# Strassen output projection: contiguous column halves and 4 KB rows for the weight sums

## The chip, the cores and the metric

One core of a Trainium2 chip runs the whole program once per launch. The metric is device time in microseconds (us). Before the change three runs took 857.10, 857.14 and 857.69 us, with a median of 857.14 us. TensorE runs at its 2.4 GHz level; the profile lists the granted clock as 0.998 of it over the span.

## The reference, cut to what matters

One decoder layer on 512 tokens of width 2048, all in float32. `y_att` comes from an attention, `y_conv` from a convolution module; the change touches only the projection that follows.

```python
h = _rmsnorm(x, g_pre)
proj = h @ w_in
...
y = jnp.concatenate([y_att, y_conv], axis=-1) @ w_out      # (512, 2048) @ (2048, 2048)
x = x + _rmsnorm(y, g_post)
```

## The kernel before

**Precision.** A float32 matrix is split into a high part `h_...` (rounded by ScalarE, L104) and a low part `l_...` (the rest, by VectorE, L105). A product then takes three matmuls, high by high, high by low and low by high (L351 to L353, L1089 to L1091).

**Steps.** The weights are taken in steps of 1 MB each. For a step SyncE issues the load into a `raws` buffer (two of them), ScalarE makes the high part, VectorE the low part, and TensorE then reads both. VectorE's instruction is the last reader of the raw buffer, so the load two steps later waits for it. Loads, splits and matmuls of all steps are ordered by the program's priorities; within an engine instructions run in order.

**The output projection by Strassen.** `w_out` is seen as 2 x 2 blocks. Rows fall into a first and a last half (`r`), columns into two classes (`c`). Before, class `c` holds column groups of 512 that alternate: group `2 * p + c` for `p` = 0, 1 (`w_block`, L978). Seven products `q` replace eight; their order is `ORDER` = 1, 5, 6, 3, 2, 7, 4 (L976). Products 1, 3 and 2 take a block of `w_out` as it is (`PLAIN`, L512). Products 5, 6, 7 and 4 take a sum of blocks (`SUMS`, L511). Each product has four steps `(p, kg)`: `p` is the column group, `kg` the half of the rows. So there are 28 steps of 24 matmuls, 16 of them on sums. A load is named `r_w` with the digits of q, p and kg, as `r_w501`. In product 4 the step (1, 0) only holds its weights, and step (1, 1) multiplies with both, 12 matmuls of each in turn (L1101 to L1121).

**The sums.** They are made by DMA alone, in DRAM tiles `ws`. `plan_sums` (L514) makes for each of 5, 6, 7, 4 four copies (L528), from `w_out` or from an earlier sum's tile, and then four accumulating transfers (L524), one for each `(p, kg)`. A transfer from `w_out` takes 512 rows of 2 KB. GpSimd issues them. `sum_next` (L536) ties each one behind the latest matmul, so that they spread over the steps from `SUMS_FROM` = 20 on; none is released in the gate steps called `z`. A sum's tile is 128 partitions x 8 KB, and `load_w` (L1003) brings it into the raw buffer in one transfer whose rows are 8 KB.

**The end.** `product_done` (L1026) combines the products into four column pieces `e` of 512 for each group `m` of 128 tokens; `finish` (L1135) scales them and adds the residual. For m < 3 two of the four pieces are scaled on ScalarE and added on GpSimd (L1174, L1175), the other two are done on VectorE (L1177); SyncE stores the four in order of `e` (L1180), between the last loads of weights.

Of the kernel before, what the change touches and what calls it, by code (L numbers as in the profile page):

```python
# [11 lines left out]
F32 = mybir.dt.float32  # L12
F32R = mybir.dt.float32r
AF = mybir.ActivationFunctionType
ALU = mybir.AluOpType

P = 128
S = 512
# [35 lines left out]
def hybrid_layer(  # L54
# [15 lines left out]
    nc = tc.nc  # L70
# [10 lines left out]
    dram = ctx.enter_context(tc.tile_pool(name="dram", bufs=1, space=bass.MemoryType.DRAM))  # L81
# [90 lines left out]
    rows = []  # L172
# [338 lines left out]
    SUMS = {5: ((0, 0), (0, 1)), 6: (5, (1, 1)), 4: (6, (1, 0)), 7: ((0, 1), (1, 1))}  # L511
    PLAIN = {1: (0, 0), 3: (1, 1), 2: (1, 0)}  # L512

    def plan_sums(name, order, pairs, block):  # L514

        made, todo = {}, deque()
        for q in order:
            base, more = SUMS[q]
            for accumulate in (False, True):
                for p in range(pairs):  # L520
                    for kg in range(2):
                        def go(q=q, base=base, more=more, accumulate=accumulate, p=p, kg=kg):
                            if accumulate:
                                return nc.gpsimd.dma_start(  # L524
                                    made[q, p, kg], block(*more, p, kg), accum_op=ALU.add
                                )
                            made[q, p, kg] = dram.tile([P, 4, S], F32, name=f"{name}{q}{p}{kg}")
                            return nc.gpsimd.dma_start(  # L528
                                made[q, p, kg],
                                made[base, p, kg] if isinstance(base, int)  # L530
                                else block(*base, p, kg),
                            )
                        todo.append(go)
        return made, todo
# [429 lines left out]
    yg, xr, gp = {}, {}, {}  # L964
    ssy = const.tile([P, NT, 4], F32, name="ssy")
# [11 lines left out]

    def w_block(r, c, p, kg):  # L978
        rows = slice((r * 2 + kg) * S, (r * 2 + kg + 1) * S)
        cols = slice((2 * p + c) * S, (2 * p + c + 1) * S)  # L980
        return w_out[rows, cols].rearrange("(k p) c -> p k c", p=P)

    w_sum, w_sumq = plan_sums("ws", (5, 6, 7, 4), 2, w_block)

    sumq = deque()
    while w_sumq:
# [16 lines left out]
    def load_w(q, p, kg):  # L1003
        name = f"w{q}{p}{kg}"
        n = ORDER.index(q)
        if (p, kg) == (1, 0) and n + 1 < len(ORDER):
            make_form(ORDER[n + 1])
        ahead = min(2000, tc.cur_priority - floor[0])
        with tc.high_priority(offset=ahead):
            raw = raws.tile([P, 4, S], F32, tag="raw", name=f"r_{name}")  # L1010
            nc.sync.dma_start(raw, w_block(*PLAIN[q], p, kg) if q in PLAIN else w_sum[q, p, kg])
            hi, lo = parts(name)
            split(hi, lo, raw)
        return hi, lo
# [3 lines left out]
    def keep(tag, m, e, name):  # L1018
        yg[m, e] = t2(f"{name}{m}_{e}")
        return yg[m, e]  # L1020
# [5 lines left out]
    def product_done(q, p, i):  # L1026

        m1, m2 = i, 2 + i
        a, b = banks.get(("a", p, i)), banks.get(("b", p, i))
        tt = nc.vector.tensor_tensor  # L1030
        if q == 1:
            nc.scalar.copy(keep("s1", m1, 2 * p, "s1_"), a)
        elif q == 5:
            nc.scalar.copy(keep("t5", m2, 2 * p + 1, "t5_"), b)
        elif q == 6:
            nc.scalar.copy(keep("r", m1, 2 * p + 1, "r_"), a)
        elif q == 3:
            c12 = yg[m1, 2 * p + 1]
            tt(out=c12, in0=b, in1=c12, op=ALU.subtract)
            done(m1, 2 * p + 1)  # L1040
        elif q == 2:
            c11 = yg[m1, 2 * p]
            tt(out=c11, in0=banks["c", p, i], in1=c11, op=ALU.add)
            done(m1, 2 * p)
        elif q == 7:
            c22 = yg[m2, 2 * p + 1]
            tt(out=c22, in0=c22, in1=a, op=ALU.subtract)
            done(m2, 2 * p + 1)
        else:
            e = 2 * p  # L1050
            c21 = keep("c21", m2, e, "c21_")
            square_sum(m2, e, a)
            scaled = partial(nc.vector.tensor_tensor, out=c21, in0=a, in1=gp[e], op=ALU.mult)
            if p == 0:
                scaled()
                sum_most(m2)
                finish(m1, 2, lambda: None)
            else:
                with tc.manual_schedule(engines={mybir.EngineType.DVE}):
                    finish(m2, 2, scaled)  # L1060
            return
        if q == 2 and p == 1:
            sum_most(m1)

    def done(m, e):
        square_sum(m, e, yg[m, e])
        nc.vector.tensor_tensor(out=yg[m, e], in0=yg[m, e], in1=gp[e], op=ALU.mult)
# [57 lines left out]
    def sum_most(m):  # L1125

        v = const.tile([P, 1], F32, name=f"fv{m}")
        nc.vector.tensor_tensor(out=v, in0=ssy[:, m, 0:1], in1=ssy[:, m, 1:2], op=ALU.add)
        nc.vector.tensor_tensor(out=v, in0=v, in1=ssy[:, m, 3:4], op=ALU.add)
        nc.vector.tensor_scalar(  # L1130
            out=v, in0=v, scalar1=-0.5 / D, scalar2=-0.5 * RMS_EPS, op0=ALU.mult, op1=ALU.add
        )
        most[m] = v

    def finish(m, left, scaled):  # L1135

        v = most[m]
# [15 lines left out]
        if m == 3:  # L1153

            ps = op2.tile([P, S], F32, tag="o2", name="last")
            diag = fin.tile([P, P], F32, name="diag")
            nc.tensor.matmul(ps, ident, xr[m][:, 0, :], start=True, stop=False)
            nc.scalar.mul(diag, ident, y)
            nc.tensor.matmul(ps, diag, yg[m, 0], start=False, stop=True)
            nc.scalar.copy(yg[m, 0], ps)  # L1160
            nc.scalar.dma_start(of[rows, :S], yg[m, 0])

            pieces = [(1, 0, S // 2), (1, S // 2, S), (3, 0, S), (2, 0, S // 2), (2, S // 2, S)]
            for n, (e, a, b) in enumerate(pieces):
                o = xr[m][:, e, a:b]
                nc.vector.scalar_tensor_tensor(
                    out=o, in0=yg[m, e][:, a:b], scalar=y, in1=o, op0=ALU.mult, op1=ALU.add
                )
                nc.sync.dma_start(of[rows, e * S + a : e * S + b], o)
            return  # L1170
        for e in range(4):
            o = xr[m][:, e, :]
            if e in (1, 3):
                nc.scalar.mul(yg[m, e], yg[m, e], y)  # L1174
                nc.gpsimd.tensor_tensor(out=o, in0=yg[m, e], in1=o, op=ALU.add)  # L1175
            else:
                nc.vector.scalar_tensor_tensor(  # L1177
                    out=o, in0=yg[m, e], scalar=y, in1=o, op0=ALU.mult, op1=ALU.add
                )
            nc.sync.dma_start(of[rows, e * S : (e + 1) * S], o)  # L1180
# [299 lines left out]
```

## Time and profile before

| what | value |
|---|---|
| runs | 857.10, 857.14, 857.69 us (median 857.14) |
| the profiled execution, its own time | 858.71 us |
| its span, first to last instruction | 857.0 us |
| share of the span: TensorE, VectorE, ScalarE, GpSimd | 99%, 77%, 49%, 16% |
| DMA, mean over the span | 228 GB/s, 195.04 MB |
| copies and accumulating transfers from w_out into ws | 24 of 1 MB, 9.4 us from issue to landing (median) |
| loads of ws tiles | 16 of 1 MB |

The profiled execution took 858.71 us where the median of the runs is 857.14; 1.71 us of it lie outside the span. Matmuls are pipelined, so a busy TensorE in these views means that it never ran dry; two matmuls with 512 columns start 0.23 us apart. Idle time of another engine matters only where TensorE waits in turn.

### The profile page before, as it was taken

The numbers are of one execution on the slowest core, as the hardware profiler recorded it, in microseconds if no ns is written. First come the engines' busy times: TensorE is split into PE (matmuls) and PEld (weight loads), VectorE is DVE, ScalarE is ACT, GpSimd is POOL, SyncE is SP. The second block draws the span as 40 slices with busy tenths as digits, with TensorE's granted clock in tenths as the row PEclk, the third lists the DMA queues.
The fourth block names the chain that finished last, engine by engine and source line by source line (L and its number), as shares of the span: only waits on it lengthen the run. The fifth ranks groups of instructions, "written<-read, shape, count | busy, mean of one in ns | idle before, by whom it ended". The sixth has DMA issues, their size and how long they took to land.

```text
span 857.0 us, 9935 instructions
## 1 busy us (share of the span) xinstructions
PE 847.6 (99%) x3872; PEld 702.3 (82%) x3872; DVE 658.5 (77%) x791; ACT 417.3 (49%) x475; POOL 137.6 (16%) x170
## 2 busy tenths in 40 slices
PE   9999999999999999999999999999999999999996
PEld 7888878888888888888888888888888888888885
DVE  5698899777589798997969898468964776458774
ACT  6784222565534342436432535369843356455543
POOL 0111110010130223222121333330000100000031
PEclk9999999999999999999999999999999999999999
DMA  8798989575877879876689887937755995557783
GB/s 317 243 289 196 325 256 234 191 225 196 299 229 209 245 148 215 276 197 196 191 222 188 235 245 159 283 103 289 295 197 197 220 263 205 197 197 260 288 282 102
DMA packets 92278, 195.04 MB, mean 228 GB/s; under 512 B 3702, under 2 KB 46210, under 8 KB 86856
## 3 DMA queue, kind: packets, MB, share of 16 engines
q1 hardware_dynamic: 66688, 120.74, 41.0%
q0 software_dynamic: 22304, 69.21, 33.7%
q10 hardware_dynamic: 3240, 4.46, 1.5%
q8 instruction: 30, 0.49, 0.2%
q14 instruction: 16, 0.13, 0.0%
HBM read 186.01 MB, written 75.50 MB: 305 GB/s over the span
## 4 chain that ended last, share of the span: by engine, by line
PE 91%; DMA 4%; DVE 2%; ACT 2%; issue 0%; POOL 0%; ACTq 0%; DVEq 0%; POOLq 0%
PE za L351 3%; PE za L353 3%; PE a L1089 3%; PE za L352 3%; PE a L1090 3%; PE a L1091 3%; PE k L353 3%; PE k L351 3%; PE k L352 3%; PE u L351 3%; PE u L353 3%; PE u L352 3%; PE q L353 3%; PE q L351 3%; PE q L352 3%; DMA r_q<-in_w_in_dram 2%
## 5 line engine op out<-in xcount | busy, mean ns | idle before, releaser
L410 DVE SCALAR_TENSOR_TENSOR acc<-hg,vec,acc 128x512 f32<-128x512 f32 x240 | 183.1, 763 | 7.2
L105 DVE TENSOR_TENSOR l_w<-r_w,h_w 128x2048 fp32r<-128x2048 f32 x28 | 64.2, 2292 | 43.5 <-ACT h_w L104 43.5
L104 ACT ACTIVATE h_w<-r_w 128x2048 fp32r<-128x2048 f32 x28 | 53.6, 1916 | 43.4 <-DMA r_w<-ws 16.9
L353 PE MATMUL k<-h_hi,l_k 128*128 128x512 f32 x128 | 50.0, 390 | 1.1 <-DVE l_k L105 1.1
L351 PE MATMUL u<-h_hi,h_u 128*128 128x512 f32 x128 | 50.1, 392 | 0.0
L351 PE MATMUL q<-h_hi,h_q 128*128 128x512 f32 x128 | 50.1, 392 | 0.0
L351 PE MATMUL za<-h_hi,h_za 128*128 128x512 f32 x128 | 50.1, 391 | 0.0
L351 PE MATMUL k<-h_hi,h_k 128*128 128x512 f32 x128 | 50.1, 391 | 0.0
L353 PE MATMUL q<-h_hi,l_q 128*128 128x512 f32 x128 | 49.9, 390 | 0.0
L353 PE MATMUL za<-h_hi,l_za 128*128 128x512 f32 x128 | 49.9, 390 | 0.0
L353 PE MATMUL u<-h_hi,l_u 128*128 128x512 f32 x128 | 49.9, 390 | 0.0
L352 PE MATMUL u<-h_lo,h_u 128*128 128x512 f32 x128 | 49.8, 389 | 0.0
L352 PE MATMUL za<-h_lo,h_za 128*128 128x512 f32 x128 | 49.8, 389 | 0.0
L352 PE MATMUL q<-h_lo,h_q 128*128 128x512 f32 x128 | 49.8, 389 | 0.0
L352 PE MATMUL k<-h_lo,h_k 128*128 128x512 f32 x128 | 49.8, 389 | 0.0
L1091 PE MATMUL a<-h_w,f_lo 128*128 128x512 f32 x128 | 49.8, 389 | 0.0
L1089 PE MATMUL a<-h_w,f_hi 128*128 128x512 f32 x128 | 49.8, 389 | 0.0
L1090 PE MATMUL a<-l_w,f_hi 128*128 128x512 f32 x128 | 49.8, 389 | 0.0
L105 DVE TENSOR_TENSOR l_z<-r_z,h_z 128x2048 fp32r<-128x2048 f32 x14 | 32.1, 2291 | 16.3 <-ACT h_z L104 16.3
L105 DVE TENSOR_TENSOR l_v<-r_v,h_v 128x2048 fp32r<-128x2048 f32 x14 | 32.1, 2290 | 15.3 <-ACT h_v L104 15.3
L698 POOL TENSOR_SCALAR_AFFINE_SELECT t<-t 128x128 f32<-128x128 f32 x64 | 33.6, 562 | 54.1 <-ACT t L734 30.1
L104 ACT ACTIVATE h_v<-r_v 128x2048 fp32r<-128x2048 f32 x14 | 26.8, 1916 | 29.6 <-PE g L352 13.2
(381 smaller groups left out, 2238.2 us busy)
## 6 DMA issues: line engine op xcount, KB each, us to landing
ws<-in_w_out_dram POOLq DMA_DIRECT2D x24, 1024.0 KB, 9.4
r_w<-ws SPq DMA_DIRECT2D x16, 1024.0 KB
vs<-in_w_in_dram POOLq DMA_DIRECT2D x12, 1024.0 KB, 12.7
zs<-in_w_in_dram POOLq DMA_DIRECT2D x12, 1024.0 KB, 9.3
r_w<-in_w_out_dram SPq DMA_DIRECT2D x12, 1024.0 KB
r_u<-in_w_in_dram SPq DMA_DIRECT2D x8, 1024.0 KB
r_q<-in_w_in_dram SPq DMA_DIRECT2D x8, 1024.0 KB
r_k<-in_w_in_dram SPq DMA_DIRECT2D x8, 1024.0 KB
```

The costliest lines, as they stand in the source:

```text
L104: nc.scalar.activation(hi, src, AF.Copy)
L105: made = nc.vector.tensor_tensor(out=lo, in0=src, in1=f32(hi), op=ALU.subtract)
L351: nc.tensor.matmul(ps, wh, ah, start=first, stop=False)
L352: nc.tensor.matmul(ps, wh, al, start=False, stop=False)
L353: latest[0] = nc.tensor.matmul(ps, wl, ah, start=False, stop=last).ins
L410: bgq.append(lambda j=j: nc.vector.scalar_tensor_tensor(out=acc, in0=hg[:, j : j + S], scalar=vec[:, ct, j : j + 1], in1=acc, op0=ALU.mult ...
L698: nc.gpsimd.affine_select(out=blk, in_=blk, compare_op=ALU.is_gt, fill=0.0, base=0, pattern=[[-1, P]], channel_multiplier=1,)
L1089: nc.tensor.matmul(ps, fh[:, kk, ts], hi[:, k, :], start=st, stop=False, skip_group_check=True)
L1090: nc.tensor.matmul(ps, fh[:, kk, ts], lo[:, k, :], start=False, stop=False, skip_group_check=True)
L1091: nc.tensor.matmul(ps, fl[:, kk, ts], hi[:, k, :], start=False, stop=en, skip_group_check=True)
```

## The change

The columns of `w_out` are split into the first and the last 1024 instead of alternating groups of 512. Class `c`, group `p` is now the column group `2 * c + p`. A sum over a class is therefore contiguous over 1024 columns, and the four tiles of a sum are cut by rows instead of by `p`: a tile `(part, kg)` holds 256 rows of 4 KB (`w_wide`) in the place of 512 rows of 2 KB. The load of step `(p, kg)` then needs half of each of two tiles, and takes two transfers of 512 KB, each with rows of 2 KB. Column pieces change their numbers: `2 * p + c` becomes `2 * c + p`, in the combining, in the sums of squares and at the end, where GpSimd now adds the pieces 2 and 3 instead of 1 and 3.

```diff
-    def plan_sums(name, order, pairs, block):
+    def plan_sums(name, order, pairs, block, shape=(4, S)):
...
-                            made[q, p, kg] = dram.tile([P, 4, S], F32, name=f"{name}{q}{p}{kg}")
+                            made[q, p, kg] = dram.tile([P, *shape], F32, name=f"{name}{q}{p}{kg}")
...
     def w_block(r, c, p, kg):
         rows = slice((r * 2 + kg) * S, (r * 2 + kg + 1) * S)
-        cols = slice((2 * p + c) * S, (2 * p + c + 1) * S)
+        cols = slice((2 * c + p) * S, (2 * c + p + 1) * S)
         return w_out[rows, cols].rearrange("(k p) c -> p k c", p=P)
 
-    w_sum, w_sumq = plan_sums("ws", (5, 6, 7, 4), 2, w_block)
+    def w_wide(r, c, part, kg):
+
+        first = r * 2 * S + kg * S + part * 2 * P
+        rows = w_out[first : first + 2 * P, c * 2 * S : (c + 1) * 2 * S]
+        return rows.rearrange("(k p) c -> p k c", p=P)
+
+    w_sum, w_sumq = plan_sums("ws", (5, 6, 7, 4), 2, w_wide, (2, 2 * S))
...
-            nc.sync.dma_start(raw, w_block(*PLAIN[q], p, kg) if q in PLAIN else w_sum[q, p, kg])
+            if q in PLAIN:
+                nc.sync.dma_start(raw, w_block(*PLAIN[q], p, kg))
+            else:
+                for part in range(2):
+                    nc.sync.dma_start(
+                        raw[:, 2 * part : 2 * part + 2],
+                        w_sum[q, part, kg][:, :, p * S : (p + 1) * S],
+                    )
...
-            e = 2 * p
+            e = p
...
-                finish(m1, 2, lambda: None)
+                finish(m1, 1, lambda: None)
...
-            if e in (1, 3):
+            if e in (2, 3):
                 nc.scalar.mul(yg[m, e], yg[m, e], y)
                 nc.gpsimd.tensor_tensor(out=o, in0=yg[m, e], in1=o, op=ALU.add)
```

On TensorE, VectorE and ScalarE the same instructions stand in the same order as before. On GpSimd the order is the same too, with other shapes. This is its stretch at the first sums of product 5 (zs is another sum, which is not touched):

```order
 L528 DMA zs_1847<-in_w_in_dram 512x1x512
-L528 DMA ws_1883<-in_w_out_dram 512x1x512
+L528 DMA ws_1883<-in_w_out_dram 256x1x1024
 L528 DMA zs_1901<-in_w_in_dram 512x1x512
-L528 DMA ws_1945<-in_w_out_dram 512x1x512
+L528 DMA ws_1945<-in_w_out_dram 256x1x1024
```

All 24 transfers from w_out change in this way; the 8 copies from one ws tile to another stay as they are.

On SyncE 147 rows become 163. At the loads of product 5 they were (r_w500 is the load of q = 5, p = 0, kg = 0; ws510 the tile of q = 5, second place, kg = 0):

```order
L1011 DMA r_w111_5325<-in_w_out_dram 128x4x512
L1011 DMA r_w500_5357<-ws500_1883 128x2048
L1011 DMA r_w501_5391<-ws501_1945 128x2048
L1011 DMA r_w510_5441<-ws510_2073 128x2048
L1011 DMA r_w511_5475<-ws511_2193 128x2048
```

and are now

```order
L1018 DMA r_w111_5325<-in_w_out_dram 128x4x512
L1021 DMA r_w500_5357<-ws500_1883 128x2x512
L1021 DMA r_w500_5357<-ws510_2073 128x2x512
L1021 DMA r_w501_5392<-ws501_1945 128x2x512
L1021 DMA r_w501_5392<-ws511_2193 128x2x512
L1021 DMA r_w510_5443<-ws500_1883 128x2x512
L1021 DMA r_w510_5443<-ws510_2073 128x2x512
L1021 DMA r_w511_5478<-ws501_1945 128x2x512
L1021 DMA r_w511_5478<-ws511_2193 128x2x512
```

Each load is two transfers, and the first load of a product now reads a tile that only the third one read before.

On SyncE at the loads of product 4, between the stores of the finished rows (xr0, xr1), it was

```order
L1011 DMA r_w400_6127<-ws400_4154 128x2048
L1180 DMA out_0_dram<-xr0_6195 128x512 x2
L1011 DMA r_w401_6165<-ws401_4183 128x2048
L1180 DMA out_0_dram<-xr0_6195 128x512 x2
L1180 DMA out_0_dram<-xr1_6197 128x512
L1011 DMA r_w410_6199<-ws410_4241 128x2048
L1180 DMA out_0_dram<-xr1_6197 128x512 x3
L1011 DMA r_w411_6283<-ws411_4972 128x2048
```

and is now

```order
L1021 DMA r_w400_6139<-ws400_4154 128x2x512
L1021 DMA r_w400_6139<-ws410_4241 128x2x512
L1193 DMA out_0_dram<-xr0_6209 128x512 x2
L1021 DMA r_w401_6178<-ws401_4183 128x2x512
L1021 DMA r_w401_6178<-ws411_4972 128x2x512
L1193 DMA out_0_dram<-xr0_6209 128x512 x2
L1193 DMA out_0_dram<-xr1_6211 128x512
L1021 DMA r_w410_6213<-ws400_4154 128x2x512
L1021 DMA r_w410_6213<-ws410_4241 128x2x512
L1193 DMA out_0_dram<-xr1_6211 128x512 x3
L1021 DMA r_w411_6298<-ws401_4183 128x2x512
L1021 DMA r_w411_6298<-ws411_4972 128x2x512
```

The stores stand at the same places, but the first two of a row, pieces 0 and 1, are now both VectorE's; before, piece 1 was GpSimd's.

## Rows read from the trace of the kernel before

**Rows 1.** The page, part 1: busy time, share of the span and instructions of each engine

```profile
PE 847.6 (99%) x3872; PEld 702.3 (82%) x3872; DVE 658.5 (77%) x791; ACT 417.3 (49%) x475; POOL 137.6 (16%) x170
```

**Rows 2.** The waits of TensorE, whole span: total us, times, longest us

```profile
PE idle L1283 <- POOL mean_w L140: 1.8, 1, 1.8
PE last L1159 <- ACT diag L1158: 1.5, 1, 1.5
PE k L353 <- DVE l_k L105: 1.1, 1, 1.1
```

**Rows 3.** Windows: length, busy PE, PEld, DVE, ACT, POOL, clock, DMA share, GB/s

```profile
0.00:20.00 20.00, 18.23 (x78) 13.95 (x79) 10.26 (x20) 12.28 (x23) 2.05 (x11) 1.00 0.86 311
...
224.00:696.00 472.00, 472.00 (x2195) 395.06 (x2194) 375.26 (x403) 221.62 (x207) 105.13 (x132) 1.00 0.78 220
696.00:848.00 152.00, 152.00 (x672) 125.84 (x672) 101.55 (x118) 81.89 (x105) 10.59 (x6) 1.00 0.63 225
```

**Rows 4.** Tile ws: issues with ns min/median/max, first and last start; landing

```profile
L524 POOL DMA_DIRECT2D ws<-in_w_out_dram x16: 1139/1170/1204, 283.5 to 685.6; - x16
...
DMA to landing us min/median/max: 5.4/8.8/12.6
```

**Rows 5.** Timeline (start, us): TensorE's first product step; load r_w501 and its use

```profile
696.04 0.39 PE L1089 MATMUL a<-h_w,f_hi 128*128 128x512 f32 x1
...
709.98 0.33 SPq L1011 DMA_DIRECT2D r_w<-ws  x1
...
716.09 1.92 ACT L104 ACTIVATE h_w<-r_w 128x2048 fp32r<-128x2048 f32 x1 [5.66 <-DMA r_w<-ws]
...
718.04 2.29 DVE L105 TENSOR_TENSOR l_w<-r_w,h_w 128x2048 fp32r<-128x2048 f32 x1 [5.28 <-ACT h_w L104]
...
723.47 0.39 PE L1090 MATMUL b<-l_w,f_hi 128*128 128x512 f32 x1
```

**Rows 6.** Timeline: load r_w511, its issue and ScalarE's start on it

```profile
720.36 0.32 SPq L1011 DMA_DIRECT2D r_w<-ws  x1
...
725.52 1.92 ACT L104 ACTIVATE h_w<-r_w 128x2048 fp32r<-128x2048 f32 x1 [2.29 <-DMA r_w<-ws]
```

**Rows 7.** DMA queue 1, packets, MB, share: 707:743 (ws loads), then 744:782 (w_out loads)

```profile
q1 hardware_dynamic: 1018, 7.42, 56.7%
...
q1 hardware_dynamic: 3696, 7.34, 56.4%
```

**Rows 8.** Timeline of SyncE at the start: four transfers of 256 KB in a row

```profile
1.25 1.84 SPq L1248 DMA_DIRECT2D r_gn<-in_w_in_dram  x4
```

**Rows 9.** Timeline at product 4: loads r_w401, r_w411 and stores

```profile
810.35 1.41 DVE L1177 SCALAR_TENSOR_TENSOR xr<-s,fy,xr 128x512 f32<-128x512 f32 x2
...
811.13 5.11 SPq L1180 DMA_DIRECT2D out_dram<-xr  x2
...
812.43 2.29 DVE L105 TENSOR_TENSOR l_w<-r_w,h_w 128x2048 fp32r<-128x2048 f32 x1 [0.67 <-ACT h_w L104]
...
816.41 0.33 SPq L1011 DMA_DIRECT2D r_w<-ws  x1
...
823.04 1.92 ACT L104 ACTIVATE h_w<-r_w 128x2048 fp32r<-128x2048 f32 x1 [1.84 <-DMA r_w<-ws]
...
827.31 0.33 SPq L1011 DMA_DIRECT2D r_w<-ws  x1
...
834.65 1.92 ACT L104 ACTIVATE h_w<-r_w 128x2048 fp32r<-128x2048 f32 x1 [2.74 <-DMA r_w<-ws]
...
836.60 2.29 DVE L105 TENSOR_TENSOR l_w<-r_w,h_w 128x2048 fp32r<-128x2048 f32 x1 [2.37 <-ACT h_w L104]
...
840.43 0.39 PE L1090 MATMUL a<-l_w,f_hi 128*128 128x512 f32 x1
```

**Rows 10.** The page, part 3: DMA queue, packets, MB, share of 16 engines

```profile
q1 hardware_dynamic: 66688, 120.74, 41.0%
q0 software_dynamic: 22304, 69.21, 33.7%
```

More of the change, by code (lines that the diff above doesn't have):

```diff
@@ L1031, in product_done @@
         if q == 1:
-            nc.scalar.copy(keep("s1", m1, 2 * p, "s1_"), a)
+            nc.scalar.copy(keep("s1", m1, p, "s1_"), a)
         elif q == 5:
-            nc.scalar.copy(keep("t5", m2, 2 * p + 1, "t5_"), b)
+            nc.scalar.copy(keep("t5", m2, 2 + p, "t5_"), b)
         elif q == 6:
-            nc.scalar.copy(keep("r", m1, 2 * p + 1, "r_"), a)
+            nc.scalar.copy(keep("r", m1, 2 + p, "r_"), a)
         elif q == 3:
-            c12 = yg[m1, 2 * p + 1]
+            c12 = yg[m1, 2 + p]
             tt(out=c12, in0=b, in1=c12, op=ALU.subtract)
-            done(m1, 2 * p + 1)
+            done(m1, 2 + p)
         elif q == 2:
-            c11 = yg[m1, 2 * p]
+            c11 = yg[m1, p]
             tt(out=c11, in0=banks["c", p, i], in1=c11, op=ALU.add)
-            done(m1, 2 * p)
+            done(m1, p)
         elif q == 7:
-            c22 = yg[m2, 2 * p + 1]
+            c22 = yg[m2, 2 + p]
             tt(out=c22, in0=c22, in1=a, op=ALU.subtract)
-            done(m2, 2 * p + 1)
+            done(m2, 2 + p)
         else:
-            e = 2 * p
+            e = p
             c21 = keep("c21", m2, e, "c21_")
@@ L1056, in product_done @@
                 sum_most(m2)
-                finish(m1, 2, lambda: None)
+                finish(m1, 1, lambda: None)
             else:
                 with tc.manual_schedule(engines={mybir.EngineType.DVE}):
-                    finish(m2, 2, scaled)
+                    finish(m2, 1, scaled)
             return
@@ L1127, in sum_most @@
         v = const.tile([P, 1], F32, name=f"fv{m}")
-        nc.vector.tensor_tensor(out=v, in0=ssy[:, m, 0:1], in1=ssy[:, m, 1:2], op=ALU.add)
+        nc.vector.tensor_tensor(out=v, in0=ssy[:, m, 0:1], in1=ssy[:, m, 2:3], op=ALU.add)
         nc.vector.tensor_tensor(out=v, in0=v, in1=ssy[:, m, 3:4], op=ALU.add)
@@ L1161, in finish @@
             nc.scalar.dma_start(of[rows, :S], yg[m, 0])
-            pieces = [(1, 0, S // 2), (1, S // 2, S), (3, 0, S), (2, 0, S // 2), (2, S // 2, S)]
+            pieces = [(2, 0, S // 2), (2, S // 2, S), (3, 0, S), (1, 0, S // 2), (1, S // 2, S)]
             for n, (e, a, b) in enumerate(pieces):
```

## The prediction

> **What bounds the kernel now.** I read the page first. TensorE is busy for 847.6 us of a span of 857.0 [rows 1], so all its idle time is 9.4 us. Then the waits of TensorE: only three are listed, 1.8 us at the very start, 1.1 us for the low part of an early weight `k`, and 1.5 us in the last computation of the kernel [rows 2]. None of them names a weight `w` of the output projection. Then the windows, to see where the idle time can lie at all. From 224 to 696 us, the stretch in which the sums of w_out are made, TensorE is busy for 472.00 of 472.00 us; from 696 to 848 us, the stretch of the seven products, for 152.00 of 152.00 [rows 3]. The reader is to see that both stretches which the change touches are already full. A transfer that gets cheaper there gives TensorE nothing; one that gets dearer costs nothing until the lead of the weights over TensorE is used up. So the question is the size of that lead.
>
> **The sums.** Twenty-four transfers change from 512 rows of 2 KB to 256 rows of 4 KB. Sixteen accumulate, the first is issued at 283.5 and the last at 685.6 us, an issue holds GpSimd for 1.17 us, and a transfer into ws lands 8.8 us after it (5.4 to 12.6) [rows 4]. With half the rows the issue should take between half of that and all of it, and the transfer hold the DMA engines no longer than now. I book nothing for either: GpSimd is busy 16% of the span [rows 1], and what the DMA engines save lies under the full 472 us of TensorE [rows 3]. A bound below zero is excluded for the same reason: no wait is there to be shortened. A bound above: the trace has no accumulating transfer with 4 KB rows. Were each to take the longest landing seen instead of the median, it would be 3.8 us later; the nearest deadline is the first load of product 4, which now reads a tile whose accumulation is among the last (685.6). That load comes ahead of the stores at 811 us [rows 4, 9], so more than 100 us lie between. The cost is nothing at both ends.
>
> **The loads of sums.** Sixteen loads of 1 MB become two transfers of 512 KB each, with rows of 2 KB instead of 8 KB. The rows first. In 707 to 743 us the queue carried ws loads in 8 KB rows, 7.42 MB at 56.7% of sixteen engines over 36 us, which is 327 engine-us or 44.0 per MB. In 744 to 782 us it carried w_out loads in 2 KB rows, 7.34 MB at 56.4% over 38 us, 343 engine-us or 46.7 per MB [rows 7]. The difference, 2.7 / 16, is 0.2 us a load. Then the second issue. Four transfers in a row were issued in 1.84 us, 0.46 us each [rows 8], so the second half starts that much later. Together I take 0.6 us more from issue to landing. The low end is 0.2 us, if the first half's data cover the second issue; the high end is in the rivals.
>
> Is there room for 0.6 us? Take r_w501. It is issued at 709.98, ScalarE starts at 716.09 after waiting for this DMA (6.11 us), VectorE ends at 718.04 + 2.29 = 720.33 [rows 5]. Its first use: a step is 24 matmuls, and 672 of them fill the 152.00 us of the products [rows 3], 0.226 us each. The products begin at 696.04 and this is the sixth load, so its step begins 120 matmuls or some 27.2 us later. The second matmul of a step is the first to read the low part; its row there is at 723.47 [rows 5]. That is 121 matmuls after the first one, which makes the spacing 0.2267 us and a step 5.44 us. The lead is 723.47 - 720.33 = 3.1 us. For r_w511 the DMA takes 720.36 to 725.52, 5.16 us [rows 6].
>
> Whether the loss adds up over loads is a matter of the two raw buffers. One buffer is held from issue to landing (L), then 1.95 us from ScalarE's start to VectorE's, then 2.29 us, and 0.03 us to the next issue; it serves every second load, so L + 4.27 must stay within 2 x 5.44 = 10.88. The ring keeps up until **L = 6.6 us**. With L of 5.2 to 6.1 now and 0.6 more it is 5.8 to 6.7. The lead stays about as it is, and TensorE does not wait: **0 us**.
>
> **The end is the tightest place.** In product 4 the last load, r_w411, is used earlier than its turn: its step begins with 12 matmuls of r_w410, at 696.04 + 26 x 5.44 = 837.48, and reads r_w411's low part from 837.48 + 13 x 0.2267 = 840.43. VectorE finishes it at 836.60 + 2.29 = 838.89 [rows 9]. The lead is only 1.5 us. It hangs on a chain: r_w401 is issued at 816.41, lands for ScalarE at 823.04 (6.6 us), its buffer is freed by VectorE 4.2 us later, r_w411 is issued at 827.31 and lands at 834.65 (7.3 us) [rows 9]. Two loads in that chain, 0.6 us each, take 1.2 of the 1.5 us.
>
> But the change also loosens the chain. r_w401 could have gone out when its buffer was free, at 812.43 + 2.29 = 814.72. It went at 816.41, because SyncE stood before the second of two stores of xr0, whose data came from GpSimd; the two stores hold the queue from 811.13 to 816.24 [rows 9]. Now both pieces are VectorE's, and VectorE has made its two by 810.35 + 1.41 = 811.76 [rows 9]. So r_w401 should go out about 1.7 us earlier, and the lead of r_w411 become 1.5 - 1.2 + 1.7, about 2 us. If that gain does not come, 0.3 us are left. Again 0 us. GpSimd's last piece of xr0 was stored between r_w401 and r_w410 before, and still is, so r_w410 meets no store that comes later than it did.
>
> **The sum.** 0 (sums) + 0 (loads) + 0 (end; same instructions in the same order) = 0 us. On the profiled execution, 858.71 us with a span of 857.0, that leaves 858.7; the median of the runs is 857.14, 1.6 us lower, and I forecast against it: **857.1 us**.
>
> **Rival 1, slower: the halves land one after the other.** Of r_w511's 5.16 us the data themselves account for 44.0 / 16 x 1.05 = 2.9 us when all engines carry it; 2.3 us are start and completion [rows 6, 7]. If the second half began only when the first was complete, each load would pay these twice: L = 7.5 to 8.4, in the middle 7.9. That passes the 6.6 us from which the ring decides. In product 5 and 6 TensorE then loses (7.9 - 6.6) / 2 = 0.65 us a load, 8 loads 5.2, less the lead of 3.1: 2 us. At the end r_w401 and r_w411 bring 2 x 2.3 = 4.6 against 1.5 + 1.7: 1.4 us, and up to 3 without the earlier issue. Together 3.4 to 5 us, about 861.5 us. It decides as slower than 0.2% (1.7 us, about what a measurement of this kernel can tell from no change) once a load grows by some 2 us. Against it: in the first 20 us most transfers are of 256 KB, four of them were issued 0.46 us apart [rows 8], and the stretch still moved 311 GB/s [rows 3]; at 2.3 us of standing time for each 256 KB, beside 0.7 us of data, it would be below 90.
>
> The Trainium skill, page "DMA: Bandwidth & Descriptors", section "Anatomy of one DMA — SWDGE (gpsimd) path", speaks against the change here: it gives a transfer a fixed 2.0 us beside its bytes, so by its fit two halves in sequence would be 6.4 us where one whole is 4.4, an estimate of 2.0 us more for a load. The trace does not agree that small transfers queued behind each other pay it each time, by the 311 GB/s above. I give the rival 0.06, with what else could make the end late (the stores meeting r_w411's halves).
>
> **Rival 2, faster: freed DMA time reaches TensorE.** For it speaks that the DMA engines are 78% occupied while the sums run [rows 3]. Against it: the one wait on a weight, 1.1 us, falls before any sum of w_out, since the window from 224 us has none [rows 2, 3]. Even all of it gone would give 856.0, which is 0.13%, and counts as no change. More than 0.2% would need TensorE's start or end to shrink, and neither has a transfer of this change in it. 0.03.
>
> **Rival 3, the change does not do what it says.** 4 KB rows could still be cut into 2 KB packets, and the sums cost what they cost now. That gives the same 857.1 us, so it shows only in the packets: it is part of the forecast's chance.
>
> **How the numbers follow.** No change 0.91 with rival 3, slower 0.06, faster 0.03. The range is the forecast's own case: the three runs lie within 0.6 us of each other and the profiled one 1.6 above the median, so I take 0.8 below and 1.4 above, 856.3 to 858.5. Some cover for a lead that just fails (a few tenths) is in the upper side; rival 1's 861.5 is left out.
>
> **What would show it.** TensorE full again from 224 to 848 us. Queue 1's packets up from 66688 [rows 10] by 16 x (2 x (256 + 16) - (128 + 16)) = 6400 to about 73090; queue 0's from 22304 down by at least 4096 if rows travel whole, unchanged by rival 3. Loads of ws with 5.5 to 7 us to ScalarE's start. r_w401 issued near 814.8. A wait of TensorE on `l_w` or `h_w` would prove me wrong, first at 840 us, then in product 5.

## The result and the profile after

The change is slower. Over 22 runs each, its median was 861.81 us against 857.26 us for the kernel before, a ratio of 1.0045 with a 95% interval of 1.0027 to 1.0062. Ratios here and below are of the fast runs (the one of 870.56 us counts as slow), so they differ a little from the quotients of the medians. The runs of the change scatter from 857.47 to 870.56 us, where all but one of the kernel before lie between 856.92 and 857.94. Three later sessions on other occasions gave 858.83, 859.01 and 859.81 us against 857.36, 857.62 and 857.39. So the loss is 1.4 to 4.6 us, and the forecast of 857.1 us, with its range up to 858.5, is missed. The profiled execution of the first session took 869.19 us with a span of 867.5, near the long end of the runs.

The page after the change, part 1 (busy time of each engine) and part 3 (DMA queues):

```profile
PE 852.1 (98%) x3872; PEld 704.0 (81%) x3872; DVE 659.2 (76%) x791; ACT 417.2 (48%) x475; POOL 137.0 (16%) x170
...
q1 hardware_dynamic: 73088, 120.74, 41.2%
q0 software_dynamic: 18208, 69.21, 35.1%
```

The work is the same as before [rows 1, 10]; the packets changed as forecast, on queue 1 to 73088 (73090 foretold), on queue 0 down by 4096, so the 4 KB rows do travel whole. TensorE's waits, whole span, total us, times, longest us:

```profile
PE a L1103 <- DVE l_w L105: 1.8, 1, 1.8
PE idle L1296 <- POOL mean_w L140: 1.8, 1, 1.8
PE k L353 <- DVE l_k L105: 1.6, 1, 1.6
PE a L1102 <- ACT h_w L104: 1.5, 1, 1.5
PE q L353 <- DVE l_q L105: 1.5, 1, 1.5
PE last L1172 <- ACT diag L1171: 1.5, 1, 1.5
PE k L351 <- ACT h_k L104: 0.6, 1, 0.6
```

Against the list of before [rows 2] there are two kinds of new waits. Those on `h_w` and `l_w` are in the output projection, which the change touches. Those on `q` and `k` belong to early projections, which it does not touch. The windows (length, busy time of PE, PEld, DVE, ACT and POOL, granted clock, DMA share, GB/s) show where both lie:

```profile
20.00:100.00 80.00, 78.46 (x379) 64.24 (x378) 65.03 (x136) 46.17 (x85) 10.63 (x12) 1.00 0.92 262
100.00:120.00 20.00, 19.04 (x83) 15.12 (x81) 16.97 (x21) 4.80 (x4) 1.69 (x2) 1.00 1.03 270
120.00:224.00 104.00, 102.80 (x444) 84.27 (x445) 83.69 (x86) 46.15 (x45) 5.96 (x6) 0.98 0.66 204
224.00:696.00 472.00, 472.00 (x2196) 395.05 (x2195) 374.93 (x401) 223.33 (x208) 105.40 (x133) 1.00 0.81 219
696.00:848.00 152.00, 149.78 (x659) 123.14 (x657) 99.63 (x110) 80.16 (x101) 8.24 (x4) 1.00 0.72 233
848.00:857.00 9.00, 7.81 (x27) 6.38 (x28) 5.55 (x15) 2.54 (x8) 0.70 (x1) 0.81 0.00 0
```

While the sums are made TensorE is as full as before [rows 3]. The products, full before, now lose 2.2 us up to 848 us, and more behind it. Where TensorE waits in them is the last load, r_w411, in the timeline (start, us, engine, line):

```profile
835.74 1.18 SPq L1021 DMA_DIRECT2D r_w<-ws  x2
...
844.90 1.91 ACT L104 ACTIVATE h_w<-r_w 128x2048 fp32r<-128x2048 f32 x1 [4.10 <-DMA r_w<-ws]
846.84 2.29 DVE L105 TENSOR_TENSOR l_w<-r_w,h_w 128x2048 fp32r<-128x2048 f32 x1 [3.72 <-ACT h_w L104]
846.86 0.51 PE L1102 MATMUL a<-h_w,f_hi 128*128 128x512 f32 x1 [1.50 <-ACT h_w L104]
849.19 0.80 PE L1103 MATMUL a<-l_w,f_hi 128*128 128x512 f32 x1 [1.82 <-DVE l_w L105]
849.78 0.63 PE L1104 MATMUL a<-h_w,f_lo 128*128 128x512 f32 x1
850.21 0.63 PE L1102 MATMUL a<-h_w,f_hi 128*128 128x512 f32 x1
```

The load takes 844.90 - 835.74 = 9.2 us to ScalarE, where it took 7.3 [rows 9]. ScalarE waits for the DMA, VectorE for ScalarE, TensorE for both. After the two waits the matmuls start 0.43 us apart (849.78 and 850.21) instead of 0.23: the granted clock of 848 to 857 us is 0.81 on average, part of it at the 1.2 GHz level (before, the products were over by then), so in this execution the waits cost more than their own length. In the other traces of the change the clock does not fall there (1.00 from 841 to 850 us in the fourth).

To keep the two kinds of lateness apart, each trace below is read in two stretches: up to the issue of the first w_out load, and from there to the end of the span. In the trace of before the first load goes out at 665.9 us and the span is 857.0, which leaves **191.1 us**. After the change it goes out at 670.5 and the span is 867.5: 4.6 us more in the first stretch, and **197.0 us**, 5.9 more, in the second. What SyncE spends on a load, before and after (tile r_w; ns min/median/max, first and last start), is new too:

```profile
L1011 SPq DMA_DIRECT2D r_w<-ws x16: 319/323/339, 703.3 to 827.3; - x16
L1011 SPq DMA_DIRECT2D r_w<-in_w_out_dram x12: 367/368/384, 665.9 to 782.2; - x12
```

```profile
L1021 SPq DMA_DIRECT2D r_w<-ws x32: 517/578/756, 709.8 to 836.3; - x32
L1018 SPq DMA_DIRECT2D r_w<-in_w_out_dram x12: 367/368/392, 670.5 to 788.5; - x12
```

One issue of 0.32 us has become two of 0.52 and 0.60, though each moves half as much.

### The profile page after: what moved, and what is told of

Its sections match the earlier page's. It is cut to its first block, busy times and chain, and to the rows that moved or that the text cites. A ratio compares the mean times of both kernels' runs of the same rounds, so it can differ in the third digit from the quotient of the medians.

```text
span 867.5 us, 9963 instructions
## 1 busy us (share of the span) xinstructions
PE 852.1 (98%) x3872; PEld 704.0 (81%) x3872; DVE 659.2 (76%) x791; ACT 417.2 (48%) x475; POOL 137.0 (16%) x170
## 3 DMA queue, kind: packets, MB, share of 16 engines
q1 hardware_dynamic: 73088, 120.74, 41.2%
q0 software_dynamic: 18208, 69.21, 35.1%
## 4 chain that ended last, share of the span: by engine, by line
PE 72%; DMA 15%; DVE 7%; ACT 4%; issue 1%; SPq 0%; ACTq 0%; POOL 0%; DVEq 0%; POOLq 0%
DMA r_w<-ws 7%; DVE l_w L105 4%; PE za L351 3%; PE za L353 3%; PE za L352 3%; DMA r_w<-in_w_out_dram 3%; PE k L353 3%; PE k L351 3%; PE k L352 3%; ACT h_w L104 3%; PE u L352 3%; PE u L353 3%; PE u L351 3%; PE q L353 3%; PE q L351 3%; PE q L352 3%
## 5 line engine op out<-in xcount | busy, mean ns | idle before, releaser
L351 PE MATMUL k<-h_hi,h_k 128*128 128x512 f32 x128 | 50.9, 398 | 0.6 <-ACT h_k L104 0.6
```

The source lines that it names most:

```text
L351: nc.tensor.matmul(ps, wh, ah, start=first, stop=False)
```

## The experiments

No kernel leaves any part of the computation out. "Lead" is the time from VectorE's end on r_w411 to TensorE's first use of its low part.

### The parts one by one

**The change again** (no edit).

> The change itself once more, nothing left out, for a second trace of it. If the change is what moves the time: a median near 861 us, ratio 1.003 to 1.006, and again TensorE waits of 1 to 2 us on l_w and h_w of r_w411 near 842 to 850 us, with a stretch of granted clock 0.5 behind them. The rival, that the lateness between 96 and 125 us of the profiled run (4.6 us) belongs to the change too, expects it here again; if it is chance, TensorE is full in 120:224 as in the kernel before and the span is 3 to 5 us shorter than that of the first trace.

Median 858.83 us (12 runs, 857.40 to 862.99), ratio 1.0025 (1.0010 to 1.0040). The wait on `l_w` is there, 0.7 us; the early ones are not: the first w_out load goes out at 664.5, and 192.1 us are left to the end of the 856.7 us span. The wait is shorter than the 1 to 2 us expected, and no stretch of the lower clock follows it. The early lateness does not belong to every run of the change.

**One transfer to a load**, against the change: the two row parts of a sum share one DRAM buffer.

```diff
-                for part in range(2):
-                    nc.sync.dma_start(
-                        raw[:, 2 * part : 2 * part + 2],
-                        w_sum[q, part, kg][:, :, p * S : (p + 1) * S],
-                    )
+                nc.sync.dma_start(raw, w_both[q, kg][:, :, p * S : (p + 1) * S])
```

> The change with both row parts of a sum in one DRAM buffer, so that the load of a sum is again one transfer of 1 MB, in rows of 2 KB. If the second issue is what makes the loads late (SyncE issues of 0.52 and 0.60 us in place of one of 0.32): loads land as in the kernel before, no wait of TensorE on r_w411, ratio 0.999 to 1.001. If the 2 KB rows are (49 engine-us for a MB in place of 44): loads take 6.5 to 9 us to ScalarE in the last products as in the change, TensorE waits on r_w411, ratio 1.003 to 1.006.

857.67 us, ratio 1.0003 (0.9992 to 1.0013), no wait, 191.1 us. It speaks for the issue and against the rows. But the lead is only 0.2 us, and this one issue is not cheap either (0.52 us):

```profile
L1031 SPq DMA_DIRECT2D r_w<-ws x16: 517/518/622, 702.3 to 825.4; - x16
```

**Two transfers alone**, against the kernel before, whose sums stay as they were:

```diff
+                for part in range(2):
+                    nc.sync.dma_start(
+                        raw[:, 2 * part : 2 * part + 2], w_sum[q, p, kg][:, 2 * part : 2 * part + 2]
+                    )
```

> The kernel before with the load of a sum in two transfers of 0.5 MB, each of 4 KB rows, nothing else changed. If the second issue is what makes the loads late: as late as in the change, 7 to 9 us to ScalarE in the last products, TensorE waits of 1 to 2 us on r_w411, ratio 1.003 to 1.006. If the 2 KB rows are: loads 0.3 to 0.6 us later than before at most, no wait, ratio 0.999 to 1.001.

857.36 us, ratio 1.0003 (0.9988 to 1.0018), no wait, lead 1.3 us, 191.1 us. So the second transfer alone is not it either. Rival 1 falls here in its purest form. The rule of the Trainium skill that stood beside it (page "DMA: Bandwidth & Descriptors", section "Anatomy of one DMA — SWDGE (gpsimd) path"), by which each half would pay a fixed 2.0 us, is given there for transfers that GpSimd issues; this run does not bear it out for two halves that follow each other on SyncE's queue.

**The columns alone**, against the kernel before: `w_block` with `2 * c + p` and the new numbers of the pieces, sums and loads as before.

```diff
-        cols = slice((2 * p + c) * S, (2 * p + c + 1) * S)
+        cols = slice((2 * c + p) * S, (2 * c + p + 1) * S)
```

> The change's split of the columns into first and last 1024, with the sums and their loads as in the kernel before (512 rows of 2 KB, one load of 1 MB). Whichever of the issue or the rows it is: ratio 0.999 to 1.001, and no wait on r_w411. If instead the new order of the last residual blocks, or the output's columns, makes the end late: ratio 1.003 to 1.006 here. r_w401 is to be issued as early as its buffer lets it, since VectorE and not GpSimd ends the last block of xr0.

857.20 us, ratio 0.9984 (0.9965 to 1.0003), no wait, 191.1 us. The timeline at the end:

```profile
813.16 0.33 SPq L1017 DMA_DIRECT2D r_w<-ws  x1
...
819.06 6.42 POOL L1181 TENSOR_TENSOR xr<-r,xr 128x512 f32<-128x512 f32 x2 [3.52 <-ACT r L1180]
...
820.81 5.03 SPq L1186 DMA_DIRECT2D out_dram<-xr  x3
...
821.72 2.60 DVE L105 TENSOR_TENSOR l_w<-r_w,h_w 128x2048 fp32r<-128x2048 f32 x1 [0.70 <-ACT h_w L104]
...
825.94 0.37 SPq L1017 DMA_DIRECT2D r_w<-ws  x1
...
833.96 1.92 ACT L104 ACTIVATE h_w<-r_w 128x2048 fp32r<-128x2048 f32 x1 [4.79 <-DMA r_w<-ws]
```

r_w401 goes out at 813.16, which on the clock of the trace of before (1.6 us later) is 814.8, exactly as forecast. Its buffer is free at 821.72 + 2.60 = 824.32. Yet r_w411 goes out only at 825.94, because SyncE stands before three stores of xr1 until 825.84, and GpSimd's piece for them ends at 825.48. The 1.7 us gained at xr0's stores are lost again at xr1's; r_w411's lead is 0.6 us, less than before.

### Where along the loads

Neither part alone waits, both together do. Is it the last product, or the lead that products 5 to 7 lose? Both kernels keep both parts of a sum in one buffer; `step` is 2 rows of blocks in product 4 alone, or everywhere but there.

**The change a third time**, on the chip of the three kernels that follow.

> The change a third time, beside the three kernels below on one chip. The change as a whole: ratio 1.002 to 1.005, runs scattered over 857.4 to 863 us, and TensorE waiting on r_w411's parts, by 0.5 to 2 us. If the two sessions so far differed by chance alone (4.5 and 1.5 us over the kernel before), the third median lies between them.

859.01 us, ratio 1.0032 (1.0014 to 1.0050), a wait of 0.7 us on `l_w`, 192.1 us to the end. It lies between the first two sessions (861.81 and 858.83), close to the lower.

**Halves in product 4 only**, against one transfer:

```diff
+                step = 2 if q == 4 else 4
+                for k in range(0, 4, step):
+                    nc.sync.dma_start(
+                        raw[:, k : k + step], w_both[q, kg][:, k : k + step, p * S : (p + 1) * S]
+                    )
```

> Loads of sums as one transfer in rows of 2 KB in products 5, 6 and 7, and as two transfers of half the size in product 4 alone. If the second issue costs only where the raw buffers' ring and the last products' traffic leave no lead, product 4 is enough: leads of 6 us and more up to product 7, then 7.5 to 9 us from issue to ScalarE in product 4, a wait on r_w411, ratio 1.001 to 1.004 as in the change. If the lead that products 5, 6 and 7 lose is needed too: no wait or one below 0.3 us, ratio 0.999 to 1.001.

857.67 us, ratio 0.9999 (0.9983 to 1.0016), no wait, lead 1.75 us.

**Halves everywhere but in product 4** (`step = 4 if q == 4 else 2`):

> The mirror of it: two transfers to a load in products 5, 6 and 7, one transfer in product 4, all in rows of 2 KB. If product 4 alone is what costs: no wait of TensorE on r_w411 or one below 0.3 us, ratio 0.999 to 1.001. If the lead lost before it is: leads of 2 to 4 us at product 4's start, a wait of 0.5 us or more on r_w411, ratio 1.001 to 1.004.

857.69 us, ratio 0.9996 (0.9984 to 1.0007), no wait, lead 1.2 us. Neither kernel waits: halves of this kind cost nothing in either place. But they are not the halves of the change, as the timeline of the first of the two kernels shows at r_w411:

```profile
825.92 0.89 SPq L1033 DMA_DIRECT2D r_w<-ws  x2
```

Two halves are issued in 0.89 us here, and in 1.18 in the change. They have the same size, the same 2 KB rows and the same target. What differs is where the rows lie. In the change a part has a buffer of its own with 8 KB for each partition, and a half takes from it 2 KB out of every 4 KB, at one even pitch through all partitions: 256 rows, 4 KB apart. In the common buffer a partition has 16 KB, and the half takes two rows 4 KB apart and then leaves two out: the pitch is uneven. One transfer of all four rows of the common buffer is again even, 512 rows 4 KB apart, and took 0.52 us. Loads of w_out are uneven, and take 0.37. A kernel with the change's own halves in product 4 alone, or everywhere but there, was not made.

**The last residual load later**, against the change: xr3, 1 MB behind r_w411 on SyncE, waits until ScalarE has read r_w411.

```diff
+            if (q, p, kg) == (4, 1, 1):
+                landed = nc.scalar.activation(hi, raw, AF.Copy)
...
+                    load_residual(3).ins, landed.ins.name,
```

> The change with one thing moved: the last residual load (xr3, 1 MB), issued right behind r_w411's two halves, is issued only when ScalarE has read r_w411. If it is that megabyte, moved in the same microseconds, that makes r_w411's halves land late: r_w411 takes 6 to 7 us from issue to ScalarE in place of 8.8 to 9.2, no wait on it, ratio 0.999 to 1.001. If the two issues and the rows alone are what takes the time, or the stores: 8 us or more still, a wait, ratio 1.001 to 1.004. If xr3 then comes too late for the last block's first matrix product: a wait of TensorE on xr near 845 us and a longer end.

858.72 us, ratio 1.0019 (1.0000 to 1.0039), a wait of 1.8 us on `l_w`, 8.4 us for r_w411, 193.3 us to the end. The megabyte of xr3 is not what makes it late. The three other residual loads stay where they were, so the loads of the sums themselves and what stands beside them on the queue remain.

### The pitch

**The change, padded**: 64 bytes behind each partition's 8 KB (`pad` is 16 float32 values), nothing else in the program.

```diff
-                            made[q, p, kg] = dram.tile([P, *shape], F32, name=f"{name}{q}{p}{kg}")
+                            k, c = shape
+                            flat = dram.tile([P, k * c + pad], F32, name=f"{name}{q}{p}{kg}")
+                            made[q, p, kg] = flat[:, : k * c].rearrange("p (k c) -> p k c", k=k)
```

> The change with 64 bytes of padding behind each partition's 8 KB of a sum's DRAM buffer and nothing else: two parts, two transfers, rows of 2 KB, the same order. Then the 256 rows of a half no longer lie at one even pitch over partitions (in the change 4 KB from row to row and from partition to partition). If it is that pattern which makes each issue of a half take 0.52 and 0.6 us (halves of one common buffer, which have no even pitch, took 0.36 to 0.47): issues of 0.36 to 0.47 us here, 0.9 us for a load in place of 1.17, loads of 5 to 5.8 us to ScalarE in products 5 and 6, no wait on r_w411, ratio 0.999 to 1.001. If two transfers in rows of 2 KB are enough whatever the pattern: issues may be shorter, but a wait on r_w411 and a ratio of 1.002 to 1.004.

**857.26 us, ratio 1.0000 (0.9991 to 1.0009)**: the loss is gone. SyncE's issues, and r_w411 in the timeline:

```profile
L1023 SPq DMA_DIRECT2D r_w<-ws x32: 359/400/1338, 702.2 to 826.2; - x32
```

```profile
825.74 0.96 SPq L1023 DMA_DIRECT2D r_w<-ws  x2
...
833.65 1.92 ACT L104 ACTIVATE h_w<-r_w 128x2048 fp32r<-128x2048 f32 x1 [3.35 <-PE a L1106]
835.60 2.29 DVE L105 TENSOR_TENSOR l_w<-r_w,h_w 128x2048 fp32r<-128x2048 f32 x1 [2.98 <-ACT h_w L104]
```

By this trace it is TensorE (`a`) and no longer the DMA that ends ScalarE's idle time before this load (in the second trace of this kernel, below, it is the DMA again). TensorE waits for no weight of the output projection, the lead is 1.2 us, and 191.1 us are left from the first w_out load to the end. The padding does two more things: the eight copies between tiles of ws go in more packets (queue 0 carries 19104, in the change 18208), and GpSimd's accumulating issues take 1.16 us instead of 1.05. Both lie in the stretch of the sums, where TensorE is full with and without them.

**Halves in one buffer, in all products** (one transfer's kernel with two transfers to each load):

> Both parts of a sum in one DRAM buffer as in the run with one transfer, but each load in two transfers of half the size, in all products. The pattern theory: the pitch of a half is uneven, so issues of 0.36 to 0.47 us, ratio 0.999 to 1.001, r_w411's lead 0.5 to 2 us. The theory that both changes of the load together (two transfers, and rows of 2 KB) use up the lead in all four products: ratio 1.002 to 1.004, with a wait on r_w411, although products 5 to 7 alone and product 4 alone did not show it.

857.49 us, ratio 1.0008 (0.9999 to 1.0018), no wait, lead 1.0 us, 191.1 us; r_w411's two issues took 0.93 us. This kernel has no padding, and its partitions lie 16 KB apart, a power of two. So it is not that padding breaks a power of two. The Trainium skill has such a rule (page "DMA: Bandwidth & Descriptors", section "Latency and other measured facts"): row pitches of 2 MB and more in powers of two lose bandwidth, 4 KB of padding restores it and 192 bytes do not. The pitches here are 4 to 16 KB, so no run here tests that rule, and the 64 bytes that help are another matter.

**One transfer, padded** (64 bytes behind each partition's 16 KB):

> The run with one transfer to a load, with 64 bytes of padding behind each partition's 16 KB, so that its 512 rows lie at an uneven pitch too. If the pattern makes the issue dear: one issue of 0.36 to 0.38 us (as w_out's loads, 512 rows of 2 KB, 0.37) in place of 0.52; ratio 0.998 to 1.001, r_w411's lead above the 0.2 us of the even pitch. If the issue is dear for any load of rows that are parts of wider ones in a sum's buffer: 0.52 us again.

The issue falls from 0.52 to 0.36 us, as the pattern theory says, and r_w411's lead is 1.3 us. The median is 858.20 us, ratio 1.0019 (1.0001 to 1.0036), which the theory does not say. TensorE's waits in its trace (the two left out stand in every trace, at the start and in the last computation), and SyncE's issues:

```profile
PE q L351 <- ACT h_q L104: 2.6, 1, 2.6
...
PE q L353 <- DVE l_q L105: 1.6, 1, 1.6
```

```profile
L1032 SPq DMA_DIRECT2D r_w<-ws x16: 359/363/378, 708.5 to 832.2; - x16
L1030 SPq DMA_DIRECT2D r_w<-in_w_out_dram x12: 367/368/378, 671.0 to 787.4; - x12
```

No wait in the output projection and 862.1 - 671.0 = 191.1 us to the end: all of this execution's lateness, 6.7 us against the quiet traces, came before the first w_out load.

### Does the early lateness belong to the change?

Three kernels on one chip.

> The change beside two padded kernels on one chip. Two stretches are read apart in its trace: up to the first load of w_out (issued at 664 us in the quiet traces, 670.5 in the first trace of the change), and from there to the end (191.1 us in traces without a wait on r_w411; 192.1, 192.2 and 197.0 in those of the change). If the even pitch costs at the end alone: 192 us or more from that load to the end here, and a lateness before it that is as likely in any of the three kernels; median 1.2 to 2 us above the kernel before. If the change also makes the loads of 90 to 125 us late: the first load of w_out after 665.5 us here and not in the padded kernel with two transfers.

The change: 859.81 us (858.35 to 867.94), ratio 1.0034 (1.0016 to 1.0051). The first w_out load goes out at 664.4, early lateness none; of a span of 858.0 there are 193.6 us to the end, and the wait is back:

```profile
828.41 1.18 SPq L1021 DMA_DIRECT2D r_w<-ws  x2
...
837.00 1.92 ACT L104 ACTIVATE h_w<-r_w 128x2048 fp32r<-128x2048 f32 x1 [3.96 <-DMA r_w<-ws]
838.51 0.39 PE L1104 MATMUL a<-h_w,f_lo 128*128 128x512 f32 x1
838.95 2.29 DVE L105 TENSOR_TENSOR l_w<-r_w,h_w 128x2048 fp32r<-128x2048 f32 x1 [3.58 <-ACT h_w L104]
838.97 0.49 PE L1102 MATMUL a<-h_w,f_hi 128*128 128x512 f32 x1
841.30 0.50 PE L1103 MATMUL a<-l_w,f_hi 128*128 128x512 f32 x1 [1.83 <-DVE l_w L105]
841.64 0.40 PE L1104 MATMUL a<-h_w,f_lo 128*128 128x512 f32 x1
```

By their starts the matmuls at 838.97, 841.30 and 841.64 lie 0.46, 2.33 and 0.34 us behind the one ahead, where 0.23 is usual. That is some 2.45 us lost, and it accounts for the 2.5 us by which 193.6 exceeds 191.1; the listed wait of 1.83 us only counts from the end of the matmul ahead.

> The change with its buffers padded, again: ratio 0.999 to 1.001, 191.1 us from the first load of w_out to the end, no wait on r_w411, if the pitch is the whole cause. A median 1 us or more above the kernel before would say that the first result of this kernel was luck.

The padded change: 857.56 us, ratio 1.0010 (0.9994 to 1.0026), no wait on r_w411, lead 1.0 us, 191.1 us to the end.

> The kernel with one padded transfer again, whose first session had 5 of 12 runs above 860.9 us with no wait on r_w411 in its trace but 4 us of waits near 100 us. If that was chance: median 857.2 to 857.7, at most 2 of 12 runs above 860.5. If the placement of the larger padded buffers makes early loads late: again 4 or more of 12, and the first load of w_out after 665.5 us in the trace of a late run.

One padded transfer: 857.35 us (857.11 to 858.18), ratio 0.9995 (0.9987 to 1.0004), first w_out load at 664.3, 191.1 us to the end. None of 12 runs above 860.5, where the same kernel had 5 of 12 in the session before. So its early lateness then came and went with the session, and the kernel before has it too: of its 30 runs here two are above 860 us. But late runs as such are more frequent in the change: 24 of its 58 runs in four sessions are above 860.5 us, and 12 of 151 of the kernel before. How many of them were late early and how many at the end, runs without a trace do not tell. So that the change also makes the early lateness more frequent is neither shown nor excluded.

| kernel | transfers, rows of a load | SyncE on r_w411, us | its lead, us | first w_out load to end, us |
|---|---|---|---|---|
| before | 1, contiguous | 0.33 | 1.5 | 191.1 |
| columns alone | 1, contiguous | 0.37 | 0.6 | 191.1 |
| two transfers alone | 2, of 4 KB | 0.83 | 1.3 | 191.1 |
| one padded transfer (second session) | 1, of 2 KB, uneven | 0.38 | 0.8 | 191.1 |
| one transfer | 1, of 2 KB, even | 0.52 | 0.2 | 191.1 |
| halves everywhere but in product 4 | in product 4: 1, of 2 KB, even | 0.53 | 1.2 | 191.4 |
| halves in product 4 only | in product 4: 2, of 2 KB, uneven | 0.89 | 1.75 | 191.4 |
| change, padded | 2, of 2 KB, uneven | 0.96 | 1.2 | 191.1 |
| halves in one buffer | 2, of 2 KB, uneven | 0.93 | 1.0 | 191.1 |
| change (four traces) | 2, of 2 KB, even | 1.18 to 1.46 | waits of 0.7 to 3.3 | 192.1 to 197.0 |
| change, last residual load later | 2, of 2 KB, even | 1.18 | a wait of 1.8 | 193.3 |

Leads of like kernels differ by up to 1 us: 1.3 and 0.8 in the two traces of one padded transfer, 0.2 and 1.2 in the two kernels whose r_w411 is one even transfer. So it is the waits, and not the leads, that set the change apart: all five traces with two even transfers to a load have one, none of the eleven others has.

No version beats the kernel before; with TensorE full there is nothing for it to gain.

## Why the prediction was wrong

**Right.** The sums cost nothing: 472.00 of 472.00 us in their stretch, and the packets are those foretold. Two transfers as such, the new columns and the new order of the pieces cost nothing, each alone. TensorE would wait, if anywhere, for r_w411 first, and that is where it waits. In products 5 and 6 the 0.6 us a load was enough: from issue to ScalarE the loads took 5.8 us on average before and 6.0 to 6.35 in the four traces of the change.

**Wrong: "Two loads in that chain, 0.6 us each, take 1.2 of the 1.5 us."** From issue to ScalarE r_w401 and r_w411 took 14.0 us together before [rows 9], and 16.8 to 18.1 in the four traces of the change: 2.8 to 4.1 us more, which is more than the lead. The 0.6 us came from four transfers at the start (0.46 us for the second issue, [rows 8]) and from 2 KB rows of w_out (0.2 us, [rows 7]), whose pattern is uneven. The halves of a sum lie evenly, and for those the issues measured 0.52 + 0.60 us against 0.32 before, 0.8 us more where 0.46 were booked; the larger part of the miss comes after the issue. In the last session the loads of products 5 and 6 took 6.35 us on average in the change and 5.66 in the padded one, those of product 4 8.4 and 7.1. That is 0.7 and 1.3 us a load for the even pitch in this pair of traces; over all traces product 4 has averages of 8.0 to 8.7 us in the change and 7.1 to 7.4 in the padded one. The forecast's own bound held: past 6.6 us the ring of two raw buffers gives up lead. But it was tried on loads of product 5 alone, and the loads pass it in products 7 and 4.

**Wrong: "about 2 us" of lead at the end.** The 1.7 us at r_w401 came with the columns alone, where xr1's stores took them back at r_w411 (lead 0.6 us). In the change they did not come in full, and in two traces not at all. Counted from the first w_out load, r_w401 was to go out at 148.9 us and does so in the columns alone and in the padded change. Before it was 150.5 us, and in the four traces of the change it is 149.5, 150.0, 150.9 and 152.1. Its buffer is free late, and this begins in product 7, where residual loads stand between the loads of sums: r_w701, behind xr1's load, takes 7.3 to 8.9 us to ScalarE in the change and 6.6 to 7.0 in every kernel without a wait. The fourth trace of the change (first w_out load at 664.41), r_w701 and then the issue of r_w401:

```profile
791.52 1.17 SPq L1021 DMA_DIRECT2D r_w<-ws  x2
...
800.16 1.92 ACT L104 ACTIVATE h_w<-r_w 128x2048 fp32r<-128x2048 f32 x1 [3.69 <-DMA r_w<-ws]
...
815.26 1.47 SPq L1021 DMA_DIRECT2D r_w<-ws  x2
```

and the padded change of the same session (first w_out load at 664.90):

```profile
792.02 0.87 SPq L1023 DMA_DIRECT2D r_w<-ws  x2
...
798.63 1.92 ACT L104 ACTIVATE h_w<-r_w 128x2048 fp32r<-128x2048 f32 x1 [2.81 <-PE c L1106]
...
813.78 0.89 SPq L1023 DMA_DIRECT2D r_w<-ws  x2
```

VectorE is done with r_w411 3.3 us later in the first than in the second, and 2.0 of them are there when r_w401 is issued. What products 5 and 6 lose counts too. In two traces of the change r_w700 goes out on time or 0.4 us late, and the waits are 0.7 us; in the two others it is 1.1 and 1.6 us late, and the waits are 1.8 and 3.3. In every kernel without a wait it is on time. So the question of the last product or the lead before it has the answer "both", as far as the order in time tells; no run separates them for the even halves.

**Rival 1** had the place, but not the mechanism: a load of products 5 and 6 grew by 0.25 to 0.6 us on average, not by the 2.3 of halves that land one after the other. That its 861.5 us lies near the 861.81 of the first session is luck; the later ones had 858.8 to 859.8. Its lesson is that the price of its end (1.4 to 3 us) was about right while its chance, 0.06, was far too small. The chain had a lead of 1.5 us, and the estimate of 0.6 us a load rested on transfers of other patterns; an upper end of 1 us a load was never tried there.

**Left open.** Of the 1.3 us a load in product 4 only 0.3 are SyncE's (1.18 against 0.89 us). The rest comes after the issue. In 806 to 840 us queue 1 moved 9.42 MB at 88.1% of sixteen engines in the change, 50.9 engine-us for a MB, and 8.91 MB at 78.9% in the padded one, 48.2. Queue 1 in that window (packets, MB, share of 16 engines), first in the change:

```profile
q1 hardware_dynamic: 4150, 9.42, 88.1%
```

and in the padded change:

```profile
q1 hardware_dynamic: 3890, 8.91, 78.9%
```

That is about 5% dearer transfers at the busiest place. What makes them so, and what makes r_w701 late behind the residual load, was not tried.

## What to carry to other kernels

A transfer is priced by its pattern, not by its bytes and row length alone: before taking a price from another transfer, compare how its rows lie in memory. Where a ring of buffers leaves 1.5 us of lead at the end, book the sum of all small costs along the chain of its last loads, begin that chain where loads first share their queue with other transfers, and look at what stands there: a gain at one store may be taken by the next. A trace with unusual lateness is read in stretches, so that what the change did not touch is not put down to it.

## What was not expected of the hardware

- 64 bytes of padding behind each partition's 8 KB in DRAM cut SyncE's issue of the same two halves from 0.52 + 0.60 to 0.36 + 0.47 us, and one whole load from 0.52 to 0.36, by making the pitch of its 2 KB rows uneven. They took the loss of the change away (2.4 us in the session in which both ran).
- A contiguous load of 1 MB is issued in 0.32 us, two halves of it in 0.83: the second costs more than the first.
- The same residual loads from `x`, which the change does not touch, are issued by SyncE in 0.50 to 0.60 us in the fourth trace of the change and in 0.34 to 0.46 in the padded change beside it. What stands ahead of them in the queue differs; that this is the reason was not tried.
- An accumulating transfer from w_out holds GpSimd 1.05 us in 256 rows of 4 KB, against 1.17 in 512 of 2 KB [rows 4]. In the padded change the same 256 rows take 1.16 us, so padding the target costs the issue about as much as twice the rows. Its landing took no less time (median 9.4 us against 8.8, of all transfers into ws). The first line is of the change, the second of the padded change:

```profile
L524 POOL DMA_DIRECT2D ws<-in_w_out_dram x16: 1021/1052/1108, 288.5 to 690.2; - x16
...
L524 POOL DMA_DIRECT2D ws<-in_w_out_dram x16: 1126/1162/1248, 283.2 to 684.3; - x16
```
